# Moving the start of every large tile to a multiple of 512 bytes in a one-core float32 encoder layer

## The chip, the cores and the metric

The kernel runs on one core of one Trainium2 chip. The metric is device time in microseconds (us); lower is better. Before the change three runs gave 1567.14, 1567.76 and 1568.34 us, median 1567.76.

## What is computed

One residual layer on x of 1024 tokens by 1024 channels, float32, cut to what matters:

```
h = rmsnorm(x, g_mix)
z = h @ w_in                      # pooling channels | q | k | v
y_pool = pool_mixer(z_pool)       # trailing windows 2, 4, 8, 16, a linear map per group, a scale
y_attn = diff_attention(q, k, v)  # 8 heads, two softmax maps each, their weighted difference times v
gates  = sigmoid(h @ w_gate + b_gate)
merged = gates[:D] * (y_pool @ w_branch_pool) + gates[D:] * (y_attn @ w_branch_attn)
x = x + merged @ w_out
h2 = rmsnorm(x, g_ffn)
x = x + square(relu(h2 @ w_up)) @ w_down
```

## The kernel before

**Work.** Almost every product is done three times over: each float32 operand is split into a high part (a cast to the engine's fast float32 form, `split`, L115 to L118, ScalarE and then VectorE or GpSimd) and the remainder, and `mm3` (L120 to L125) issues high by high (L123), high by low (L124) and low by high (L125). Each of the three is a weight load of 128 by 128 and a matmul of 512, 384 or 256 moving columns. In the order of time the stages are:

- attention, head by head, with the gate (`g`) and pooling (`u`, `yp`) projections filled in between: `z` (L427, 384 columns, weights `hT`, moving `wqkv`), scores `sc` (L499 and L500, weights `Q`, moving `K`), transposes `ta` and `tk` with `identf` moving, `po` (L571, weights `V`, moving `AT`);
- branch projections `bp` (weights `wbp`, moving `ypT`) and `ba` (weights `wba`, moving `yT`), then the output projection `op` (weights `mT`, moving `wo`);
- the MLP as two block products with seven instead of eight multiplications (Strassen's form). Up: sixteen pairs `up_pair(p)`, each with products `X`, `Y`, `Z`, `W` of 12 matmuls; the weights are split pieces of `w_up` (`A`, `AS`), the moving side is one of seven combinations of h2 (`B11`, `B21`, `BT1`, `BT2`, `BT3`, `BT4`, `B22`). Down: seven products `d_product` over 8 steps of 24 matmuls, outputs `Da` and `Db`, weights `u` (reloaded up-projection results), moving `w` (split pieces of `w_down`).

**Order.** A planner fills each engine's queue from the program's priorities and from costs of its own; SyncE issues nearly all loads, ScalarE some stores. Each queue runs in order.

**Where tiles lie.** SBUF is used as two stacks per partition: pools opened without a side grow from the low end, pools opened with `side="right"` grow down from the high end. A tile takes its bytes per partition rounded up to 32, and the pools follow one another in the order in which they are opened. So the size of every small tile sets the start of all that lies above it (on the right: below it). Counted up from the sizes:

| what | starts at | beyond a multiple of 512 |
|---|---|---|
| `identf` (L227, the first tile) | 16,512 | 128 |
| `const` pool ends, `hp0` begins (L87): `identf` 512, `mhalf` 32, `ones` 512, `inv` 64, `cols` 128, `gs`, `zero` and four small tiles of the second norm 32 each | 17,952 | 32 |
| so also all of `hp0`, `hp1`, `wpool`, `rpool` and `fr`: `hT`, `ypT`, `mT`, `wqkv`, `wbp`, `wba`, `wo`, raw loads; and later on the same side `BT1` to `BT4`, `B22`, the pieces `A` and `AS`, the pieces `w` of the down projection | | 32 |
| `fo` (L139), two buffers of 528 floats, 2,112 bytes each | 144,928 | 32 and 96 |
| what follows `fo`: `fu`, `mx`, then the eleven `U` tiles (`K`, `V`, scores, `AT`, `x`, `yT`) | 149,152 on | 160 |
| small attention tiles behind them: `dist`, `qn`, `Q` | | 320, 416, 416 |
| right side, down from 229,344: `nb` (`B11`, `B21`), raw `w_up`, `y`, `gfb`; later raw `w_down` and `u` of the down projection | | 480 |

The tiles that the diff touches are `fo` (temporaries of the pooling and gate stages), `cols` (per-channel biases and scales, turned from 32 rows to columns by one transpose at L384 and copied by VectorE at L385; columns 0 to 20 are read) and the right stack, opened at L853 when the attention pools have been closed (L836).

Of the kernel before, what the change touches and what calls it, by code (L numbers as in the profile page):

```python
# [8 lines left out]
F32 = mybir.dt.float32  # L9
# [8 lines left out]
P = 128  # L18
# [15 lines left out]
N_FW, N_FR, N_FO = 4, 2, 2  # L34
# [21 lines left out]
def encoder_kernel(  # L56
# [21 lines left out]
    nc = tc.nc  # L78
# [5 lines left out]
    const = ctx.enter_context(tc.tile_pool(name="const", bufs=1))  # L84
# [6 lines left out]
    fp = mix.enter_context(tc.tile_pool(name="fp", bufs=1))  # L91
# [45 lines left out]
        return wpool.tile(shape, F32R, tag="fw", name=name, bufs=N_FW)  # L137

    def fo_tile(name):  # L139
        return fp.tile([P, 528], F32, tag="fo", name=name, bufs=N_FO)  # L140

    def fr_tile(shape, name):
        return fp.tile(shape, F32, tag="fr", name=name, bufs=N_FR)
# [90 lines left out]
    for i in range(16):  # L234
        nc.gpsimd.memset(inv[:, i : i + 1], 1.0 / (i + 1))

    cols = const.tile([P, 32], F32, name="cols")
    gs = const.tile([P, 1], F32, name="gs")
    zero = const.tile([P, 1], F32, name="zero")
    y_dram = dram.tile([D, S], F32, name="y_dram")  # L240
# [48 lines left out]
    with ExitStack() as ph:  # L289
# [92 lines left out]
        def columns():  # L382
            cols_ps = ps_t.tile([P, 512], F32, tag="tr", name="cols_ps")
            nc.tensor.transpose(cols_ps[:, 0:32], rows, identf[0:32, 0:32])  # L384
            nc.vector.tensor_copy(cols, cols_ps[:, 0:32])  # L385
            nc.vector.tensor_scalar(gs, cols[:, 20:21], 1.0 - LAMBDA_INIT, None, op0=ALU.mult)

        def small_params():
# [256 lines left out]
        for g in range(-2, N + 8):  # L645
            for t in range(4, NT):
                if LX[t] == g:
                    load_x(t)
            for t in range(1, NT):
                if NX[t] == g:  # L650
                    norm_x(t)
            if g == G_DIST:
                distances()
            if g == G_COLS:
                columns()
            gens = {}
            for tok in ORDER:
                if tok not in gens:
                    i = g - tok[1]
                    gens[tok] = stage(tok[0], i) if 0 <= i < N else iter(())  # L660
                next(gens[tok], None)
            for gen in gens.values():
                for _ in gen:
                    pass
# [35 lines left out]
    def pool_group(g):  # L700
# [7 lines left out]
        for th in range(2):  # L708
# [7 lines left out]
            while sh < win:  # L716
                nxt = fo_tile(f"sum{g}_{th}_{sh}")
                nc.gpsimd.tensor_copy(nxt[:, 0:sh], cur[:, 0:sh])
                nc.vector.tensor_tensor(nxt[:, sh:n], cur[:, sh:n], cur[:, 0 : n - sh], op=ALU.add)
                cur = nxt  # L720
                sh *= 2
# [12 lines left out]
            ps = ps_f.tile([P, 512], F32, tag="f", name=f"yp{g}_{th}")  # L734
            mm3(ps, wg[:, 0, :], wg[:, 1, :], m[:, 0, :], m[:, 1, :], True, True)
            yp = fo_tile(f"yps{g}_{th}")
            nc.scalar.activation(yp[:, 0:512], ps, AF.Copy, scale=cols[:, 16 + g : 17 + g])
            nc.scalar.dma_start(p_dram[g * P : (g + 1) * P, th * 512 : (th + 1) * 512], yp[:, 0:512])

    def gate_cols(c):  # L740
        ws = fill_w(w_gate, c * P, f"gate{c}")
        for th in range(2):
            ps = fill_proj(ws, th, f"g{c}_{th}", spare_bank if c >= G_Z else fill_bank)
            fo = fo_tile(f"go{c}_{th}")
            nc.scalar.activation(fo[:, 0:512], ps, AF.Identity, bias=cols[:, c : c + 1])
            nc.scalar.dma_start(g_dram[c * P : (c + 1) * P, th * 512 : (th + 1) * 512], fo[:, 0:512])
            yield
# [90 lines left out]
    def pool_of(stack, name, bufs, space=None, side=None):  # L838
        kw = {} if space is None else {"space": space}
        return stack.enter_context(  # L840
            tc.tile_pool(name=name, bufs=bufs, reuse_waits="tile", side=side, **kw)
        )
# [7 lines left out]
    dve, pool = nc.vector, nc.gpsimd  # L850
    hs = ctx.enter_context(ExitStack())
    norms = ExitStack()
    nb_pool = pool_of(hs, "nb", 4, side="right")  # L853
    pr1 = pool_of(hs, "pr1", N_R1, side="right")
    pr2 = [pool_of(hs, "pr20", 1, side="right")]
# [451 lines left out]
```

## Time and profile before

| | |
|---|---|
| median of three runs | 1567.76 us |
| profiled execution, first to last instruction (its span) | 1565.6 us |
| VectorE, ScalarE, GpSimd busy | 1016.4, 817.6, 357.3 us |
| weight loads busy (beside the matmuls) | 1322.5 us |
| DMA | 206.94 MB, mean 132 GB/s |

The profile is of one execution. Its own time is the span plus what lies around it; the median of the runs is 2.16 us above the span. In the views, PE is TensorE, DVE VectorE, ACT ScalarE, POOL GpSimd. A matmul's listed duration is longer than the time to the next one's start, because matmuls overlap; the pace of TensorE is therefore read from starts, or from a count in a stretch in which it is never idle.

### The profile page before, as it was taken

The page shows a single profiled execution, that of the slowest core. Times are in us where ns is not written, and L with a number is a line of the kernel's source. Part 1 is how long each engine was busy: PE and PEld are TensorE (multiplying, and loading weights), DVE is VectorE, ACT ScalarE, POOL GpSimd, SP SyncE. Part 2 cuts the span into 40 slices and gives each one's busy share as a digit, 9 for nine tenths or more (in the row PEclk, how much of TensorE's full clock was granted, in tenths as well). Part 3 has the DMA queues.
Part 4 walks back from the last instruction along what each step waited for, and adds up shares of the span by engine and source line. Part 5 has one row for each costly group of instructions (what it writes and reads, how often), then busy time and mean ns, then how long its engine had stood idle before and what let it go on. Part 6 is the DMA issues. An engine that isn't in the chain of part 4 may idle for free.

```text
span 1565.6 us, 22082 instructions
## 1 busy us (share of the span) xinstructions
PE 1536.9 (98%) x7649; PEld 1322.5 (84%) x7649; DVE 1016.4 (65%) x2277; ACT 817.6 (52%) x1810; POOL 357.3 (23%) x449
## 2 busy tenths in 40 slices
PE   7999999999999999999799999999999999999999
PEld 6899999999999989888688887888888788888887
DVE  6777677777878797743542358776666568546572
ACT  6656556656565655544542546565555634333331
POOL 5433333343434252222454400000000000000000
PEclk9999999999999999999899999999999999999999
DMA  7111212121112121256645633555342699537650
GB/s 227 50 52 48 64 46 62 34 64 52 60 44 67 35 89 40 69 158 207 205 143 177 193 115 117 182 166 185 132 141 108 247 316 381 197 121 252 218 195 27
DMA packets 168010, 206.94 MB, mean 132 GB/s; under 512 B 10118, under 2 KB 104027, under 8 KB 167899
## 3 DMA queue, kind: packets, MB, share of 16 engines
q1 hardware_dynamic: 150490, 178.23, 35.3%
q10 hardware_dynamic: 17408, 27.30, 4.7%
q8 instruction: 60, 0.98, 0.3%
q14 instruction: 52, 0.42, 0.1%
HBM read 150.94 MB, written 54.56 MB: 131 GB/s over the span
## 4 chain that ended last, share of the span: by engine, by line
PE 49%; DVE 1%; ACT 1%; DMA 1%; issue 1%; POOLq 0%; DVEq 0%
PE Da L124 4%; PE Da L123 4%; PE Da L125 4%; PE Db L124 3%; PE Db L123 3%; PE Db L125 3%; PE X L123 3%; PE X L124 3%; PE X L125 3%; PE ba L124 2%; PE op L123 2%; PE op L125 2%; PE op L124 2%; PE ba L125 2%; PE ba L123 2%; PE Z L123 2%
## 5 line engine op out<-in xcount | busy, mean ns | idle before, releaser
L123 PE MATMUL z<-wqkv,hT 128*128 128x384 f32 x512 | 174.5, 341 | 0.5 <-DVE qn L441 0.3
L125 PE MATMUL z<-wqkv,hT 128*128 128x384 f32 x512 | 174.3, 341 | 0.5 <-DVE hT L118 0.4
L124 PE MATMUL z<-wqkv,hT 128*128 128x384 f32 x512 | 173.6, 339 | 0.0
L510 ACT ACTIVATE s<-s,nm 128x256 f32<-128x256 f32 (+7 forms) x128 | 99.6, 778 | 48.9 <-DVE nm L502 44.0
L249 POOL TENSOR_TENSOR ms<-ms,mhalf 128x4 f32<-128x4 f32 x64 | 67.4, 1053 | 157.8 <-DVE ms L248 139.3
L125 PE MATMUL g<-hT,fwgate 128*128 128x512 f32 x256 | 101.0, 394 | 0.0
L124 PE MATMUL g<-hT,fwgate 128*128 128x512 f32 x256 | 100.9, 394 | 0.0
L123 PE MATMUL g<-hT,fwgate 128*128 128x512 f32 x256 | 100.9, 395 | 0.0
L123 PEld LDWEIGHTS z<-wqkv,hT 128*128 128x128 f32 x512 | 96.8, 189 | 4.2 <-DVE qn L441 1.0
L125 PEld LDWEIGHTS z<-wqkv,hT 128*128 128x128 f32 x512 | 96.6, 189 | 3.1 <-DVE hT L118 1.3
L124 PEld LDWEIGHTS z<-wqkv,hT 128*128 128x128 f32 x512 | 96.7, 189 | 2.9
L502 DVE CUSTOM_DVE_ANT_0 s<-sc,dist 128x512 f32<-128x512 f32 (+3 forms) x128 | 74.7, 586 | 22.1 <-PE sc L500 20.7
L118 DVE TENSOR_TENSOR AS<-s,AS 128x512 fp32r<-128x512 f32 x64 | 43.9, 689 | 36.7 <-ACT AS L117 36.5
L118 POOL TENSOR_TENSOR wqkv<-rqkv,wqkv 128x384 fp32r<-128x384 f32 x60 | 63.1, 1071 | 19.6 <-ACT wqkv L117 19.3
L499 PE MATMUL sc<-K,Q 128*128 128x512 f32 (+2 forms) x192 | 67.2, 355 | 0.1
L500 PE MATMUL sc<-K,Q 128*128 128x512 f32 (+2 forms) x192 | 66.6, 354 | 0.0
L473 ACT CAST Q<-tk 64x128 fp32r<-64x128 f32 x128 | 33.2, 259 | 58.6 <-DVE Q L472 56.8
L447 POOL TENSOR_TENSOR qn<-qn,ggh 128x128 f32<-128x128 f32 x64 | 32.3, 505 | 137.7 <-DVE qn L441 119.5
L470 ACT CAST Q<-tk 64x128 fp32r<-64x128 f32 x128 | 33.0, 258 | 50.1 <-DVE K L469 48.7
L123 PE MATMUL ba<-yT,wba 128*128 128x512 f32 x128 | 51.7, 404 | 7.6 <-ACT yT L117 7.6
L118 POOL TENSOR_TENSOR fwgate<-frgate,fwgate 128x512 fp32r<-128x512 f32 x32 | 45.0, 1408 | 53.7 <-ACT fwgate L117 53.5
L125 PEld LDWEIGHTS g<-hT,fwgate 128*128 128x128 f32 x256 | 48.1, 188 | 8.6
(429 smaller groups left out, 4659.6 us busy)
## 6 DMA issues: line engine op xcount, KB each, us to landing
wd<-in_w_down_dram SPq DMA_DIRECT2D x56, 512.0 KB, 5.6
wu<-in_w_up_dram SPq DMA_DIRECT2D x32, 512.0 KB, 5.0
udS<-us SPq DMA_DIRECT2D x64, 256.0 KB, 2.3
ur<-udS SPq DMA_DIRECT2D x32, 512.0 KB, 3.4
rqkv<-in_w_in_dram SPq DMA_DIRECT2D x64, 192.0 KB, 2.8
ud<-u ACTq DMA_DIRECT2D x48, 256.0 KB, 3.9
ur<-ud SPq DMA_DIRECT2D x24, 512.0 KB, 3.9
frgate<-in_w_gate_dram SPq DMA_DIRECT2D x32, 256.0 KB, 2.7
```

Source lines behind the costliest of these rows:

```text
L118: (lo_eng or nc.vector).tensor_tensor(lo, src, f(hi), op=ALU.subtract)
L123: nc.tensor.matmul(ps, lhs_hi, rhs_hi, start=first, stop=False, **kw)
L124: nc.tensor.matmul(ps, lhs_hi, rhs_lo, start=False, stop=False, **kw)
L125: nc.tensor.matmul(ps, lhs_lo, rhs_hi, start=False, stop=last, **kw)
L249: nc.gpsimd.tensor_tensor(dst, dst, mhalf[:, :n], op=ALU.pow)
L447: nc.gpsimd.tensor_tensor(qn[:, 2:4, :], qn[:, 2:4, :], ggh.unsqueeze(1).broadcast_to([P, 2, HD]), op=ALU.mult)
L470: nc.scalar.copy(q_hi, q)
L473: nc.scalar.copy(Q[other, m, 1, :], q)
L499: nc.tensor.matmul(dst, Q[:, i, 0, :], rhs, start=True, stop=False)
L500: nc.tensor.matmul(dst, Q[:, i, 1, :], rhs, start=False, stop=True)
L502: nc.vector.tensor_tensor_reduce(out=s[i][:, c : c + w], in0=sc[:, 0:w], in1=dist[:, o0 + c : o0 + c + w], scale=2.0 ** -(h + 1), scalar=B ...
L510: nc.scalar.activation(s[i][:, 0:n], s[i][:, 0:n], AF.Exp, bias=last, scale=-1.0, accum_out=Z[:, i, t : t + 1])
```

## The change

```
@@ fo_tile
-        return fp.tile([P, 528], F32, tag="fo", name=name, bufs=N_FO)
+        return fp.tile([P, 576], F32, tag="fo", name=name, bufs=N_FO)
@@ constants
-    cols = const.tile([P, 32], F32, name="cols")
+    cols = const.tile([P, 24], F32, name="cols")
@@ columns()
-            nc.vector.tensor_copy(cols, cols_ps[:, 0:32])
+            nc.vector.tensor_copy(cols, cols_ps[:, 0:24])
@@ before the right-hand pools (before line 853)
+    edge = ctx.enter_context(tc.tile_pool(name="edge", bufs=1, side="right"))
+    nc.gpsimd.memset(edge.tile([P, 120], F32, name="edge"), 0.0)
```

`cols` takes 96 bytes instead of 128, so everything above it on the left moves down by 32: `hp0` begins at 17,920, which is 35 times 512. Each `fo` buffer takes 2,304 bytes instead of 2,112, so what follows them moves up by 384 less 32: `fu` begins at 149,504, which is 292 times 512. `edge`, 480 bytes at the top of the right side, moves all right-hand tiles down by 480: they begin below 228,864, which is 447 times 512. The offsets 32, 160 and 480 of the table all become 0; `fo`'s second buffer goes from 96 to 256, `dist` from 320 to 160, `qn` and `Q` from 416 to 256. `identf`, `mhalf`, `ones` and `inv` stay. The two buffers of `fo` are used in their first 528 columns as before. One memset on GpSimd is added, of a tile that nothing reads; one VectorE copy writes 24 columns instead of 32. No other instruction is added, taken away or given another shape.

## The prediction

> **What bounds the kernel now.** I read the page first, then TensorE's waits, then busy time by stretch, then the order of time of TensorE's matmuls at several places.
>
> ```profile
> span 1565.6 us, 22082 instructions
> PE 1536.9 (98%) x7649; PEld 1322.5 (84%) x7649; DVE 1016.4 (65%) x2277; ACT 817.6 (52%) x1810; POOL 357.3 (23%) x449
> ```
>
> ```profile
> engine line waited for: us in total, times, longest us
> PE hps L275 <- DVE hn L270: 8.7, 2, 8.4
> PE ba L123 <- ACT yT L117: 7.6, 1, 7.6
> PE Z L123 <- ACT BT1h L117: 2.8, 1, 2.8
> ```
>
> ```profile
> core 0: us, PE busy (x), PEclk, DMA share, GB/s
> 660.00:742.00 82.00, 82.00 (x393) 1.00 0.53 169
> 742.00:760.00 18.00, 9.15 (x37) 0.86 0.54 173
> 760.00:860.00 100.00, 99.90 (x421) 0.97 0.57 176
> ...
> 1000.00:1230.00 230.00, 230.00 (x1007) 1.00 0.42 145
> 1260.00:1550.00 290.00, 290.00 (x1268) 1.00 0.64 220
> ```
>
> TensorE is the bound almost throughout: 1536.9 of 1565.6 us. Its waits are 8.7 us at the start, 7.6 us where the branch projections begin, 2.8 us at the start of the MLP and little else. In three long stretches (82, 230 and 290 us) it is never idle, at full clock (1.00), with DMA between 0.42 and 0.64 busy. So only two things can move the time: those waits, and the pace of matmul after matmul. The waits are loads and chains that the diff does not shorten. The pace is where tile starts could tell, and the next rows show that they may. They are starts of matmuls with 512 moving columns in one MLP pair; rows between are left out.
>
> ```profile
> start us, us, engine line op out<-in xcount [idle before <-releaser]
> 1101.31 0.39 PE L123 MATMUL Z<-B22h,AS 128*128 128x512 f32 x1
> ...
> 1104.03 0.39 PE L123 MATMUL X<-B11h,A 128*128 128x512 f32 x1
> ...
> 1106.83 0.39 PE L123 MATMUL Y<-B21h,A 128*128 128x512 f32 x1
> ...
> 1109.63 0.39 PE L123 MATMUL X<-BT2h,AS 128*128 128x512 f32 x1
> ...
> 1112.37 0.39 PE L123 MATMUL Z<-BT1h,AS 128*128 128x512 f32 x1
> ```
>
> Each product is 12 matmuls. The first, from `B22`, takes (1104.03 - 1101.31) / 12 = 0.2267 us each; those from `B11` and `B21` take 2.80 / 12 = 0.2333; the one from `BT2` takes 2.74 / 12 = 0.2283. Same shape, same engines around them. `B22` and `BT2` begin 32 bytes past a multiple of 512, as their weights do; `B11` and `B21` begin 480 past, with weights at 32. The second place is the change from one branch projection to the other:
>
> ```profile
> 741.71 0.39 PE L123 MATMUL bp<-ypT,wbp 128*128 128x512 f32 x1
> ...
> 745.11 0.40 PE L123 MATMUL ba<-yT,wba 128*128 128x512 f32 x1
> ...
> 749.07 0.39 PE L125 MATMUL ba<-yT,wba 128*128 128x512 f32 x1
> ```
>
> `bp` (both at 32) takes 3.40 / 15 = 0.2267 us; `ba` (moving `yT` at 160, weights at 32) 3.96 / 17 = 0.2329. The third is the down projection, moving at 32, weights at 480:
>
> ```profile
> 1399.64 0.39 PE L123 MATMUL Db<-w_2h,u_2h 128*128 128x512 f32 x1
> ...
> 1402.39 0.39 PE L123 MATMUL Db<-w_3h,u_3h 128*128 128x512 f32 x1
> ```
>
> 2.75 / 12 = 0.2292 us; over the long stretch quoted above it is 290 / 1268 = 0.2287. So in three stages matmuls whose two operands begin at the same offset run at 0.2267, and those with different offsets at 0.2287 to 0.2333. My reading is that the moving stream and the load of the next weights meet in the memory, and how often depends on where each begins within 512 bytes. The rows show that pairs of equal offset are the quick ones. They do not show what an offset of 0 does, since no large tile begins at 0 today.
>
> **The change part by part.** After it, moving and weight tiles of all these products begin at 0, equal offset. I take their pace to be that of the equal pair today, 0.2267. The counts:
>
> ```profile
> L123 PE MATMUL X<-B11h,A 128*128 128x512 f32 x64 | 25.3, 395 | 0.0
> L123 PE MATMUL Y<-B21h,A 128*128 128x512 f32 x64 | 25.3, 395 | 0.0
> L123 PE MATMUL Da<-w_1h,u_1h 128*128 128x512 f32 x32 | 12.5, 392 | 0.0
> L123 PE MATMUL ba<-yT,wba 128*128 128x512 f32 x128 | 51.7, 404 | 7.6 <-ACT yT L117 7.6
> ```
>
> - `X` from `B11` and `Y` from `B21`: 64 matmuls in each of three lines, two products, 384 in all, times 0.2333 - 0.2267 = 6.6 ns: 2.5 us.
> - Down projection: 7 products of 8 steps of 24 matmuls, 1,344 (the quoted group of 32 is one line of one buffer in one output). The gain per matmul is 2.0 ns by the stretch and 2.5 by the two rows; at 2.2 it is 3.0 us.
> - `ba`: 128 in each of three lines, 384, times 6.2 ns is 2.4 us; the first 10 us or so behind the 7.6 us wait run at a lowered clock (0.86 and 0.97 in the rows of the stretches), so I take 2.0.
> - `z`, `g`, `u`, `bp`, `op` and the products from `BT` and `B22`: equal before and after, 0. `po` (160 with 160) too. Scores: `K` goes from 160 to 0 and `Q` from 416 to 256, so their distance stays; 0, with at most 6 ns on its 192 matmuls of 512 columns, 1 us, either way.
>
> All of it lies on the path, since in these stages nothing else is late: gains on TensorE come straight off the span until a load is. The nearest to that is the first product of the down projection, but its average over the stage is 0.64 of the DMA engines.
>
> DMA: each 512 KB, the last number is us from issue to landing.
>
> ```profile
> ryT<-y_dram SPq DMA_DIRECT2D x8, 512.0 KB, 4.9
> ur<-ud SPq DMA_DIRECT2D x24, 512.0 KB, 3.9
> ga<-g_dram SPq DMA_DIRECT2D x8, 512.0 KB, 3.3
> ```
>
> All three are rows of 4 KB per partition into tiles at 32, 480 and 160. The tile at 32 has the slowest landing, so landings do not rank by offset; 0 is taken. Bounds from the two waits that end with a load: a tenth of 8.7 + 7.6 us, 1.6 us, either way. [...]
>
> The small edits:
>
> ```profile
> L542 POOL MEMSET AT<- 128x128 f32 x32 | 5.6, 205 | 5.6 <-PE ta L555 4.4 <-PE po L123 1.2
> L249 POOL TENSOR_TENSOR nrs<-nrs,mhalf 128x1 f32<-128x1 f32 x8 | 7.7, 967 | 60.6 <-DVE nrs L248 60.6
> 951.28 3.87 POOL L249 TENSOR_TENSOR nrs<-nrs,mhalf 128x1 f32<-128x1 f32 x1 [20.29 <-DVE nrs L248]
> ```
>
> The chain that ended last, in order of time, has that last power and then the `Z` that waited:
>
> ```profile
> 951.25 3.91 POOLq L1302
> ...
> 961.21 0.50 PE Z L123
> ```
>
> The memset of 120 columns costs about the 0.2 us of the one of 128. Nothing has used the top 480 bytes before, so it waits for nobody. Behind it in GpSimd's queue are at most the second norm's powers, for which GpSimd idles 60.6 us; that covers it. Without cover, 0.2 us. The last of those powers took 3.87 us against a mean of 0.97 for the eight, and lies in the chain ahead of the 2.8 us wait of `Z`; an instruction more on that queue could move it, by anything between -2.8 and +0.2 us; taken as 0. The copy of `cols` (L385) loses 8 of 32 columns, a few ns at most, once. The wider `fo` costs nothing but room. Which earlier tiles a new tile lies over, and so waits for, stays: right-hand tiles began 1,344 bytes into a `U` slot and now begin 512 into the same one, and everything else moves with its neighbours.
>
> Sum: 2.5 + 3.0 + 2.0 = 7.5 us off 1565.6, span 1558.1. With the 2.2 us around it unchanged: 1567.8 - 7.5 = **1560.3 us**, 0.5% faster. Two times nearer than 0.2%, 3.1 us, can't be told apart by a measurement of this kernel; that is "the same" below.
>
> **The rivals.**
>
> *Starts don't matter (19%): 1567.8.* Every slow pair above also has one operand in the upper part of the partition (`B11`, `u`, `yT`) and the other in the lower; every quick one has both below. If that distance is the cause, offsets change nothing. The rows can't separate the two, since today region and offset go together. [...]
>
> *A start at 0 is better than an equal start (18%): 1528.* Today's quick pairs are both at 32, and their pace has an unexplained constant:
>
> ```profile
> 320.23 0.33 PE L125 MATMUL z<-wqkv,hT 128*128 128x384 f32 x1
> ...
> 323.35 0.28 PE L123 MATMUL po<-AT_0h,V 128*128 128x256 f32 x1
> ```
>
> ```profile
> L123 PE MATMUL z<-wqkv,hT 128*128 128x384 f32 x512 | 174.5, 341 | 0.5 <-DVE qn L441 0.3
> ```
>
> 18 matmuls of 384 columns take 3.12 us, 0.1733 each. From 384 to 512 columns that is 53.4 ns for 128, 0.417 ns a column, and 13.3 ns are left at no column. If a start at 32 makes each stream fetch one piece of memory more than a start at 0, part of the 13.3 goes from every matmul: 512 `z` in each of three lines, 1,536, the scores of these sizes 256, and 4,632 others, 6,424 in all. At 5 ns that is 32 us: 1528. Its ends are 1 ns (1554) and 13.3 ns with the whole 7.5 (1475). Against it: nothing in the trace begins at 0.
>
> *All streams in step (9%): 1576.* Three offsets become one for every engine. The `BT2` product ran at 0.2283 and `B22`'s at 0.2267 with the same offsets, so what the other engines do costs up to 1.6 ns. If sharing one offset raises that on all matmuls of 384 and 512 columns by 2.5 ns, it costs 16 us, less the 7.5: 1576. It decides above 10.6 / 6,424 = 1.7 ns. Against it: inside the left side everything shares one offset already, and that is where the quick rows are.
>
> *The queues come out in another order (4%): 1572.* Two of the planner's costs change, and a wait like the 7.6 us one can grow; by half of it, and if the gain is absent too, 1572.
>
> **How the numbers follow.** My case has 50%; its own range is 1556 to 1564 (the scores, DMA and GpSimd bounds around 1560.3). Range for 8 in 10: 1530 to 1571. It holds my case, the case without effect, the milder part of the better one (8 of its 18%) and what lies just above; left out are a larger gain (10%) and the worst of the slower two (10%). Faster: 50 + 18 = 68%. Same: 19%. Slower: 9 + 4 = 13%.
>
> **What would show it.** In the profile after: products from `B11` and `B21` take 12 x 0.2267 = 2.72 us instead of 2.80, the stretch of 290 us in the down projection holds some 1,279 matmuls instead of 1,268, `ba` runs at 0.2267, and `B22`'s products stay at 2.72. If `B22`'s and `z`'s pace falls too, the start at 0 has a worth of its own; if nothing moves, region and not offset is the cause; if `B22`'s rises, the streams are in step. A time outside 1556 to 1564 with the paces as forecast would mean that a wait moved instead.

## The result, and the profile after

The changed kernel takes 1559.41 us (median of five runs, 1556.98 to 1560.50) against 1567.76 of the kernel before (five runs, 1566.17 to 1568.87). The ratio is 0.9945 with a 95% interval of 0.9933 to 0.9957: 8.6 us less, between 6.7 and 10.5 (the medians alone lie 8.35 apart). The forecast was 1560.3, 7.5 us less, which that interval takes in.

The order of the instructions in every queue is the same as before, apart from the one memset; TensorE's queue has two semaphore instructions fewer, which is why the count of the page falls by one. So the two traces can be laid side by side. First the page of the profile after:

```profile
span 1555.2 us, 22081 instructions
PE 1528.5 (98%) x7649; PEld 1322.9 (85%) x7649; DVE 1018.0 (65%) x2277; ACT 818.6 (53%) x1810; POOL 358.9 (23%) x450
```

The profiled execution is the fastest of the five (1556.98 us, 1.8 above its span). TensorE is busy 8.4 us less with the same 7,649 matmuls; nothing else moved by more than 2 us. The waits of TensorE after the change:

```profile
engine line waited for: us in total, times, longest us
PE hps L275 <- DVE hn L270: 10.4, 2, 9.1
PE ba L123 <- ACT yT L117: 4.8, 1, 4.8
PE Z L123 <- ACT BT1h L117: 2.8, 1, 2.8
```

The first grew by 1.7 us and the second shrank by 2.8. In the eleven other kernels below, whose queues are the same up to there, the second wait is between 5.4 and 7.3 us, so these are differences between executions, and this one was lucky by about a microsecond.

The pace, in the same places as in the prediction: one MLP pair (starts of the first matmul of each product, 12 matmuls apart), `ba` (51 matmuls between the two rows), and the long stretch of the down projection (busy time, number of matmuls, clock, DMA share, GB/s).

```profile
1116.74 0.39 PE L123 MATMUL X<-B11h,A 128*128 128x512 f32 x1
...
1119.46 0.39 PE L123 MATMUL Y<-B21h,A 128*128 128x512 f32 x1
...
1122.18 0.39 PE L123 MATMUL X<-BT2h,AS 128*128 128x512 f32 x1
...
1124.90 0.39 PE L123 MATMUL Z<-BT1h,AS 128*128 128x512 f32 x1
```

```profile
802.66 0.39 PE L123 MATMUL ba<-yT,wba 128*128 128x512 f32 x1
...
814.22 0.39 PE L123 MATMUL ba<-yT,wba 128*128 128x512 f32 x1
```

```profile
1260.00:1550.00 290.00, 290.00 (x1281) 1.00 0.61 214
```

`B11`, `B21` and `BT2` now take 2.72 us each, 0.2267 a matmul; `ba` 11.56 / 51 = 0.2267; and 1,281 matmuls fit into the stretch that held 1,268. (A count takes in one or two that are cut by the stretch's edges; by starts the pace is 226.7 ns, it was 228.9.) `z`, `g`, `u`, `op`, `bp` and the products from `B22` stay as they were.

Summed over all matmuls of 512 and 384 columns that follow without a wait, the time by which starts lie more than 226.7 and 173.3 ns apart falls from 14.6 to 6.8 us. Of the 7.8 us, the down projection gives 3.0, `B11` and `B21` 2.4, `ba` 2.1 and `BT2` 0.3. That is the measured gain, well within its interval.

### The profile page after: what moved, and what is told of

It reads as the page before. It is cut to its first block, busy times and chain, and to the rows that moved or that the text cites. A ratio compares the mean times of both kernels' runs of the same rounds, so it can differ in the third digit from the quotient of the medians.

```text
span 1555.2 us, 22081 instructions
## 1 busy us (share of the span) xinstructions
PE 1528.5 (98%) x7649; PEld 1322.9 (85%) x7649; DVE 1018.0 (65%) x2277; ACT 818.6 (53%) x1810; POOL 358.9 (23%) x450
## 4 chain that ended last, share of the span: by engine, by line
PE 50%; DVE 1%; ACT 1%; DMA 1%; issue 0%; POOLq 0%; DVEq 0%
PE Da L125 4%; PE Da L124 4%; PE Da L123 4%; PE Db L125 3%; PE Db L124 3%; PE Db L123 3%; PE X L123 3%; PE X L125 3%; PE X L124 3%; PE op L123 2%; PE op L124 2%; PE op L125 2%; PE ba L124 2%; PE ba L125 2%; PE Z L123 2%; PE ba L123 2%
## 5 line engine op out<-in xcount | busy, mean ns | idle before, releaser
L123 PE MATMUL z<-wqkv,hT 128*128 128x384 f32 x512 | 174.3, 341 | 0.3 <-DVE qn L441 0.2
L125 PE MATMUL z<-wqkv,hT 128*128 128x384 f32 x512 | 173.9, 340 | 0.0
L124 PE MATMUL z<-wqkv,hT 128*128 128x384 f32 x512 | 173.6, 339 | 0.0
L124 PE MATMUL g<-hT,fwgate 128*128 128x512 f32 x256 | 101.0, 394 | 0.0
L125 PE MATMUL g<-hT,fwgate 128*128 128x512 f32 x256 | 100.9, 394 | 0.0
L123 PE MATMUL g<-hT,fwgate 128*128 128x512 f32 x256 | 100.8, 395 | 0.0
L123 PEld LDWEIGHTS z<-wqkv,hT 128*128 128x128 f32 x512 | 96.5, 188 | 3.8 <-DVE qn L441 0.8
L124 PEld LDWEIGHTS z<-wqkv,hT 128*128 128x128 f32 x512 | 96.5, 188 | 3.2 <-POOL wqkv L118 0.2
L125 PEld LDWEIGHTS z<-wqkv,hT 128*128 128x128 f32 x512 | 96.5, 188 | 2.4 <-DVE hT L118 0.5
L123 PE MATMUL ba<-yT,wba 128*128 128x512 f32 x128 | 50.8, 397 | 4.8 <-ACT yT L117 4.8
L125 PEld LDWEIGHTS g<-hT,fwgate 128*128 128x128 f32 x256 | 48.1, 188 | 8.6
```

What stands on the lines that cost most here:

```text
L123: nc.tensor.matmul(ps, lhs_hi, rhs_hi, start=first, stop=False, **kw)
L124: nc.tensor.matmul(ps, lhs_hi, rhs_lo, start=False, stop=False, **kw)
L125: nc.tensor.matmul(ps, lhs_lo, rhs_hi, start=False, stop=last, **kw)
```

## The experiments

Three questions were open: whether equal starts or starts at 0 made the gain, whether the place in the partition had a part in it, and what the period is. Theory A: the distance between the starts of the moving tile and the weight tile within 512 bytes sets the pace. Theory B: it is the start at a multiple of 512. In all runs but the last the order of the queues is that of the kernel before, memset aside. The runs share their chips with runs of the kernel before: median 1567.81 us for the first eight, 1567.89 for the rest.

**Everything at 32.** Middle and right moved to the left's 32 (448 bytes at the right edge), `cols` as before:

```
-        return fp.tile([P, 528], F32, tag="fo", ...)
+        return fp.tile([P, 576], F32, tag="fo", ...)
...
+    edge = ctx.enter_context(tc.tile_pool(name="edge", bufs=1, side="right"))
+    nc.gpsimd.memset(edge.tile([P, 112], F32, name="edge"), 0.0)
```

> All large tiles begin at 32 past a multiple of 512: left as before, the middle moved from 160 to 32, the right from 480 to 32. Theory A (only the distance between the starts of moving and weight tile within 512 bytes counts): same time as the change, about 1559.4 us, every product of 512 columns in the MLP and ba at 0.2267 us a matmul. Theory B (a start at a multiple of 512 counts): B11 and B21 products and ba stay above 0.2267, time near 1567.8.

1560.10 us, ratio 0.9955 (0.9942 to 0.9967). In one pair `B11` takes 1124.10 - 1121.38 = 2.72 us, and the stretch of the down projection holds as many as after the change:

```profile
1121.38 0.39 PE L123 MATMUL X<-B11h,A 128*128 128x512 f32 x1
...
1124.10 0.39 PE L123 MATMUL Y<-B21h,A 128*128 128x512 f32 x1
```

```profile
1260.00:1550.00 290.00, 290.00 (x1282) 1.00 0.64 218
```

No large tile begins at a multiple of 512 and the gain is all there. Theory B falls.

**The right side alone.** Edge of 448 bytes, nothing else:

```
+    edge = ctx.enter_context(tc.tile_pool(name="edge", bufs=1, side="right"))
+    nc.gpsimd.memset(edge.tile([P, 112], F32, name="edge"), 0.0)
```

> Only the right side moves, from 480 to 32, equal to the left; the middle stays at 160. Theory A: B11, B21 and down products go to 0.2267, ba stays at 0.2324 to 0.2329; 5.5 us faster, about 1562.3. Theory B: no change, 1567.8.

1563.29 us, ratio 0.9965 (0.9951 to 0.9978), 5.5 us less, between 3.4 and 7.7. `ba` is no quicker than before, (815.63 - 803.73) / 51 = 0.2333, the stretch is quick:

```profile
803.73 0.40 PE L125 MATMUL ba<-yT,wba 128*128 128x512 f32 x1
...
815.63 0.39 PE L125 MATMUL ba<-yT,wba 128*128 128x512 f32 x1
```

```profile
1260.00:1550.00 290.00, 290.00 (x1281) 1.00 0.64 218
```

By starts `ba` takes 233.3 ns here and 232.4 before, though neither of its tiles has moved: one and the same distance gives one pace to about a nanosecond, not closer.

**The middle alone.** `fo` of 576 floats, nothing else:

```
-        return fp.tile([P, 528], F32, tag="fo", ...)
+        return fp.tile([P, 576], F32, tag="fo", ...)
```

> Only the middle (U tiles, yT) moves, from 160 to 32, by the wider fo tiles. Theory A: ba goes to 0.2267, the MLP paces stay (0.2333 and 0.2289); 2.0 to 2.4 us faster, about 1565.6. Theory B: no change, 1567.8.

1566.65 us (eleven runs), ratio 0.9994 (0.9985 to 1.0003): by time no difference that can be told, 0.9 us less with an interval from 2.4 less to 0.5 more, which takes in the forecast 2.0 and ends at the 2.4. The trace shows the step itself: `ba` at (812.84 - 801.28) / 51 = 0.2267, the stretch unchanged.

```profile
801.28 0.39 PE L125 MATMUL ba<-yT,wba 128*128 128x512 f32 x1
...
812.84 0.39 PE L125 MATMUL ba<-yT,wba 128*128 128x512 f32 x1
```

```profile
1260.00:1550.00 290.00, 290.00 (x1269) 1.00 0.64 218
```

**The left alone.** `cols` of 24 floats, so left at 0, middle at 128, right at 480:

```
-    cols = const.tile([P, 32], F32, name="cols")
+    cols = const.tile([P, 24], F32, name="cols")
...
-            nc.vector.tensor_copy(cols, cols_ps[:, 0:32])
+            nc.vector.tensor_copy(cols, cols_ps[:, 0:24])
```

> Only the narrower cols: left tiles at 0, middle at 128, right at 480. Theory A: distance right to left goes from 448 to 480, so B11, B21 and down products have a pace other than 0.2267 still; ba keeps its distance of 128 and its 0.2324 to 0.2329. Theory B in the form that the moving tile's own start counts: down products (moving at 0) go to 0.2267, B11 and B21 stay at 0.2333.

1572.22 us in one run, 4.4 more than before. A third of the change alone is a loss: the distance between left and right shrank from 64 to 32, and the down projection went not to 0.2267 but to 0.2333 (by starts 233.3 ns).

```profile
1260.00:1550.00 290.00, 290.00 (x1244) 1.00 0.65 218
```

4.4 ns on 1,344 matmuls are some 6 us. So a short distance isn't a mild one. As expected, `B11` and `B21` (now at a distance of 480) are still slow, 233.4 and 233.3 ns, and `ba` keeps its 232.4.

**Four other places of the right side.** The left stays at 32; an edge of 96, 80, 48 and 16 floats puts the right at 96, 160, 288 and 416. The edit for 96:

```
+    edge = ctx.enter_context(tc.tile_pool(name="edge", bufs=1, side="right"))
+    nc.gpsimd.memset(edge.tile([P, 96], F32, name="edge"), 0.0)
```

Right at 96:

> The kernel before with the right side at 96 instead of 480 past a multiple of 512; left at 32. Moving minus weight start is then 64 for the B11 and B21 products (it was the down projection's 64) and 448 for the down projection (it was the others' 448). Theory A: the two paces change places: B11 and B21 at 0.2289, down at 0.2333 us a matmul; 5.9 us lost and 1.7 won, about 1572. Rival (the price belongs to the product, its tiles or its place, and any distance but 0 costs it alike): 0.2333 and 0.2289 stay as they are, about 1567.8.

Right at 160:

> The right side at 160. Theory A: B11 and B21 (distance 128) run at the pace that ba has at distance 128, 0.2324 to 0.2336; the down projection (distance 384) has a pace not seen so far, which the run with the right side at 416 must show for B11 and B21. Rival: 0.2333 and 0.2289 stay.

Right at 288:

> The right side at 288, half of 512 away from the left: distance 256 both ways. Theory A: B11, B21 and the down projection have one and the same pace, whatever it is. Rival: 0.2333 and 0.2289 stay.

Right at 416:

> The right side at 416: distance 384 for B11 and B21, 128 for the down projection. Theory A: down at ba's pace, 0.2324 to 0.2336, B11 and B21 at the pace that the down projection shows with the right side at 160. Rival: 0.2333 and 0.2289 stay.

One run each: 1573.27, 1571.72, 1562.34 and 1570.87 us. The `B11` product of one pair and the stretch of the down projection, right at 96, 160, 288 and 416 in this order:

```profile
1123.51 0.40 PE L123 MATMUL X<-B11h,A 128*128 128x512 f32 x1
...
1126.27 0.40 PE L123 MATMUL Y<-B21h,A 128*128 128x512 f32 x1
...
1260.00:1550.00 290.00, 290.00 (x1244) 1.00 0.65 220
```

```profile
1122.90 0.40 PE L123 MATMUL X<-B11h,A 128*128 128x512 f32 x1
...
1125.69 0.40 PE L123 MATMUL Y<-B21h,A 128*128 128x512 f32 x1
...
1260.00:1550.00 290.00, 290.00 (x1249) 1.00 0.65 219
```

```profile
1122.31 0.39 PE L123 MATMUL X<-B11h,A 128*128 128x512 f32 x1
...
1125.03 0.39 PE L123 MATMUL Y<-B21h,A 128*128 128x512 f32 x1
...
1260.00:1550.00 290.00, 290.00 (x1281) 1.00 0.64 217
```

```profile
1121.97 0.40 PE L123 MATMUL X<-B11h,A 128*128 128x512 f32 x1
...
1124.76 0.40 PE L123 MATMUL Y<-B21h,A 128*128 128x512 f32 x1
...
1260.00:1550.00 290.00, 290.00 (x1250) 1.00 0.64 218
```

By starts, over all matmuls of each kind, in ns (moving start less weight start within 512 in brackets):

| right side at | `Y` from `B21` | down projection | run |
|---|---|---|---|
| 480 (before) | 233.3 (448) | 228.9 (64) | 1567.8 |
| 96 | 229.4 (64) | 233.3 (448) | 1573.3 |
| 160 | 233.1 (128) | 232.4 (384) | 1571.7 |
| 288 | 226.8 (256) | 226.7 (256) | 1562.3 |
| 416 | 233.2 (384) | 232.4 (128) | 1570.9 |
| 32 | 226.8 (0) | 226.7 (0) | 1563.3 |

At 96 the two paths change places to within 0.5 ns for `B21` (`B11`, which follows products at another distance, is at 230.2). At 160 and 416 the two paces should be exchanged as well: 233.1 and 232.4 at a distance of 128, 232.4 and 233.2 at 384, so again to within a nanosecond. So the price belongs to the distance, not to the product or its tiles: the rival falls. And 288 was a surprise: a distance of 256 costs nothing. The period is 256 bytes, not 512, as far as two pairs show it: 0 with 256, and 128 with 384. Distances of 192 and 320 were not run.

**Equal within 256 only.** The kernel before with 192 bytes at the edge and `fo` of 544 floats: middle and right at 288, left at 32.

```
-        return fp.tile([P, 528], F32, tag="fo", ...)
+        return fp.tile([P, 544], F32, tag="fo", ...)
...
+    edge = ctx.enter_context(tc.tile_pool(name="edge", bufs=1, side="right"))
+    nc.gpsimd.memset(edge.tile([P, 48], F32, name="edge"), 0.0)
```

> The kernel before with 192 bytes at the right edge and fo of 544 floats: left at 32, middle and right at 288, so that all starts are equal within 256 bytes and none but the left agree within 512; no large tile begins at a multiple of 256 or 512. If the rule is equal starts within 256 bytes: the full gain, about 1559.5 to 1560, and 0.2267 in the MLP and ba. If ba needs 512: 2 us less of it, about 1562.

1559.97 us (five runs), ratio 0.9951 (0.9938 to 0.9965). `ba` takes 11.56 / 51 = 0.2267:

```profile
801.80 0.39 PE L125 MATMUL ba<-yT,wba 128*128 128x512 f32 x1
...
813.36 0.39 PE L125 MATMUL ba<-yT,wba 128*128 128x512 f32 x1
```

```profile
1260.00:1550.00 290.00, 290.00 (x1281) 1.00 0.62 217
```

The full gain, with two fifths of the room at the edge and a third of the extra in `fo`, and no large tile at a multiple of 256 or 512.

**The scores too.** The changed kernel with `qn` and `Q` 256 bytes higher, so that `Q` and `K` are equal within 512:

```
-        rows = sp.tile([32, P], F32, name="rows")
+        rows = sp.tile([32, P + 64], F32, name="rows")[:, 0:P]
```

> The changed kernel with 256 bytes more in front of qn and Q, so that Q too begins at a multiple of 512 (distance to K 0 instead of 256). If the rule is equal starts within 256 bytes, as the run with the right side at 288 suggests, the scores keep 0.2313 to 0.2315 us a matmul of 512 columns and nothing changes. If it is 512 for the scores, they go to 0.2267, or to the 0.2300 of the gate products beside them, 0.3 to 0.9 us.

1562.21 us in one run. The groups of 512 columns, first of the changed kernel, then of this one (count, busy us, mean ns of one):

```profile
L499 PE MATMUL sc<-K,Q 128*128 128x512 f32 x96 | 38.8, 404 | 0.1
L500 PE MATMUL sc<-K,Q 128*128 128x512 f32 x96 | 38.1, 397 | 0.0
```

```profile
L499 PE MATMUL sc<-K,Q 128*128 128x512 f32 x96 | 38.8, 404 | 0.1
L500 PE MATMUL sc<-K,Q 128*128 128x512 f32 x96 | 38.1, 396 | 0.0
```

By starts 231.5 ns in both. Nothing moves, as it should when 256 is already as good as 0. What the scores lose beyond 226.7 they lose like `g` (230.0 ns, equal starts), in the attention stage, so unequal starts are not its cause. What is stays open.

**One weight load in three.** In the down projection of the changed kernel the four low-part weight tiles move down by 128 bytes:

```
-    puo = pool_of(ctx, "puo", 8, side="right")
+    puo = pool_of(ctx, "puo", 4, side="right")
+    gap = pool_of(ctx, "gap", 1, side="right")
+    nc.gpsimd.memset(gap.tile([P, 32], F32, name="gap"), 0.0)
+    puol = pool_of(ctx, "puol", 4, side="right")
...
+                (puol if n + x == "ul" else pool_).tile([P, 2, 512], ...)
```

> The changed kernel, with the four low-part weight tiles of the down projection moved 128 bytes down (start 384) and everything else of it at 0, so that one weight load in three has distance 128 from the moving tile. If the price is paid where the weight load runs beside the stream before it, the matmul ahead of a low-part load (high by low, L124) takes longer than 0.2267, the other two not, and the mean rises by about a third of the 5.7 ns of distance 128, 1.9 ns: about 2.6 us lost. If the price belongs to the matmul that uses those weights, it is the low by high one (L125) that takes longer. If the weights' start has no part in it (only the moving tile's place against something else), all stay at 0.2267.

1563.52 us in one run. None of the three forms of the expectation holds: by starts high by high (L123) takes 226.7 ns, high by low (L124, beside the low-part load) 232.5 and low by high (L125, which uses those weights) 234.2, together 231.1. Weights' starts have a part in it, since of all the tiles that the matmuls read they alone were moved. (The pools opened behind them, with raw loads, moved down by 128 too, and some splits and loads are queued in another order; but no matmul reads the raw loads, and the price falls on the two matmuls at the moved weights and not on the third.) But one misplaced load in three costs 4.4 ns on the mean instead of 1.9: the matmul beside it pays 5.8, about the 5.7 that distance 128 costs each matmul where all loads have it, and the next one pays 7.5 on top of its 226.7. How two such prices come from one load is not shown.

```profile
1260.00:1550.00 290.00, 290.00 (x1257) 1.00 0.62 214
```

## Why the prediction was right, point by point

- *What bounds the kernel.* Right: TensorE's busy time fell by 8.4 us and the time with it. Nothing else became late.
- *Pace of equal starts, 0.2267.* Right to the last digit that the rows have, in all three stages (by starts over all pairs, `B11` is at 227.0). That it could be carried from a pair at 32 to a pair at 0 was a choice among rivals; the run with everything at 32 shows that it was the right one.
- *`B11` and `B21` 2.5 us, down projection 3.0, `ba` 2.0.* Measured 2.4, 3.0 and 2.1. The sum had no term for `BT2`'s 0.3.
- *Scores, DMA, GpSimd at 0.* Scores: unchanged (231.3 and 231.5 ns by starts). DMA: landings of 512 KB changed little with a start at 0:

```profile
ur<-ud SPq DMA_DIRECT2D x24, 512.0 KB, 3.8
ryT<-y_dram SPq DMA_DIRECT2D x8, 512.0 KB, 5.2
ga<-g_dram SPq DMA_DIRECT2D x8, 512.0 KB, 3.2
x<-in_x_dram SPq DMA_DIRECT2D x7, 512.0 KB, 5.3
```

  against 3.9, 4.9, 3.3 and 5.4. In the wait at the start no gain can be told: TensorE's first matmul came at 9.06 us instead of 8.45, and between 8.85 and 9.42 in the five runs that leave the middle, and so the tiles of `x`, at 160. The memset took 0.19 us and ran 2.1 us after the start, since it waits for nobody; the last power is as long as it was:

```profile
L854 POOL MEMSET edge<- 128x120 f32 x1 | 0.2, 187 | 0.0
...
944.66 3.88 POOL L249 TENSOR_TENSOR nrs<-nrs,mhalf 128x1 f32<-128x1 f32 x1 [20.28 <-DVE nrs L248]
```

- *Rival, starts don't matter.* Fell: tiles stayed in their regions and the paces changed, by up to 6.7 ns in 226.7.
- *Rival, a start at 0 is better.* Fell: 226.7 ns at 0 as at 32, and with 288 against 32. The 13.3 ns that are left at no column are there at 0 as at 32 (`z`, of 384 columns, keeps its 173.3 ns).
- *Rival, all streams in step.* Fell, and its ground was a misreading. `BT2`'s 0.2283 was not the price of other engines' work. Between the rows of `BT2` that the prediction quotes lies this one of the kernel before:

```profile
1111.24 0.39 PE L124 MATMUL X<-BT2l,AS 128*128 128x512 f32 x1
```

  The first seven matmuls took (1111.24 - 1109.63) / 7 = 0.2300, the last five (1112.37 - 1111.24) / 5 = 0.2260. The slow ones are those right behind `B21`'s product: the disturbance of unequal starts lasts some matmuls into the next product (over all pairs the second to the fifth take 227.9 to 233.7 ns, the rest at most 227.0), and with `B21` mended it is gone. The run with the right side alone shows that: it leaves `BT2` and its weights where they were, and `BT2` takes 226.7 instead of 228.0.
- *Rival, another order.* Did not occur.
- *The reason given.* Half shown. That the distance of the two starts sets the pace is shown, to about a nanosecond, by the six places of the right side and by the run that is equal within 256 only. That moving stream and weight load meet in the memory is still an inference: moving one weight tile in three shows that weights' starts are a party, and that the price isn't paid by the one matmul beside the load alone. And "within 512 bytes" was too coarse; it is 256, as far as the two pairs of distances show it. This did the forecast no harm, since starts that are equal within 512 are equal within 256 too.

## What to carry to other kernels

When matmuls of one shape, back to back without waits, run at different paces in different stages, compare where their moving and weight tiles begin: here equal starts within 256 bytes were worth 0.5% of the whole, and it took only the sizes of two small tiles and a third one at the edge, with a memset of 0.19 us that nothing waits for. Move all sides or reckon each distance: moving the left side alone cost 4.4 us here, because a distance of 32 bytes is dearer than one of 64 (233.3 against 228.9 ns a matmul). Read the pace from starts or from counts in a stretch without idle time, since a listed duration hardly shows it (395 ns for `B11`, 389 for `B22` before the change).

## What the runs showed of the hardware that was not expected

- Time between starts of float32 matmuls of 512 columns, each with its own weight load of 128 columns, by distance of the two starts: 0 and 256 bytes 226.7 ns; 32 bytes 233.3; 64 bytes 228.9; 128 and 384 bytes 232.4; 448 bytes 233.3 (down projection, 1,343 intervals each). 64 and 448, equally far from equal starts on the two sides, are not alike.
- The disturbance outlasts its cause by some matmuls: `BT2` behind `B21` (0.2300 us each over its first seven, 0.2260 over the last five), and the matmul behind the misplaced load in the last experiment (234.2 ns).
- At equal starts a matmul of 512 columns takes 226.7 ns and one of 384 takes 173.3. The straight line through the two leaves 13.3 ns at no column, with starts at 0 and at 32 alike; where they come from is open.
